# TensorE's products as one loop of eight rounds, in a batched matrix product that the DMA queue bounds

## The chip, the cores and the metric

One core of a Trainium2 chip. The metric is the device time of one execution in microseconds, as the median of several. The four executions of the kernel before took 134.46 to 134.86 us, a range of 0.3%. The times of one table were taken on the same chip in the same rounds.

## The reference, cut to what matters

```python
batch, dim_i, dim_j, dim_k = 32, 256, 512, 384
x: (batch, dim_i, dim_j) float32        # 16.8 MB
y: (batch, dim_j, dim_k) float32        # 25.2 MB
out = np.einsum('bij,bjk->bik', x, y).astype(np.float32)   # 12.6 MB
```

## The kernel before

The kernel works on eight groups of four matrices. For each group, SyncE issues the loads of x and y; VectorE rounds x to 16 bits (2.29 us for 128 x 4096), transposes it (2.00 us for 128 x 1024 as 32-bit elements), and rounds y (0.95 us for 128 x 1536); TensorE makes 128 products; ScalarE (and VectorE for one or a few banks) copies the sums out of PSUM; SyncE stores the group. All data transfers go through one queue (q1, 54.53 MB), which the 16 DMA engines share: the trace has 16 completion writes for each of the 24 loads and stores, which are taken here as 16 shares, one for each engine.

```python
PLAN = """
x0 x1 y0
T0 x2 y1
T1 R0 M0 C0 x3 y2
T2 D0 R1 M1 C1 x4 y3
...                                   # cut: the same pattern
T6 D4 R5 M5 C5 y7
T7 D5 R6 M6 C6 R7 M7 C7 D7 S3 S4 S5 S6 S7
"""
x_pool, y_pool, yr_pool: bufs=2;  xr_pool: bufs=1;  xt_pool: bufs=3;  o_pool: bufs=5   # cut to sizes

def multiply(n):                      # M: one group's products, written out for every n
    for e in range(NE):               # NE = 2 halves
        for t in range(T):            # T = 16
            for g in range(Q):        # Q = 4 matrices, each on 32 partitions
                nc.tensor.matmul(ps_of[n, e, g], xt[s, e, t // 2, :, t % 2], y_r[s, t],
                                 start=(t == 0), stop=(t == T - 1))

def collect(n, vector):               # C on ScalarE, D on VectorE: PSUM -> o_sb
    ...
def store(n):                         # S: one DMA of 1.5 MB
    ...
```

The framework (a scheduler with pools of buffers) places the waits; nothing in TensorE's program branches back. TensorE's program is therefore 8 x 128 products, each with a weight load (1,024 of each on the page).

## Time and profile before

| | before |
|---|---|
| time, median of 3 | 134.52 us (134.51 to 134.86) |
| span of the profiled execution | 132.9 us |
| busiest compute engine | VectorE, 72% |
| the data queue's share of the 16 DMA engines' time | 96.9% |
| fetches of TensorE's instructions | 8, of 16 KiB each |

Read it from the queue's share down: here one resource is at 97% and every engine at 72% or less, so only that resource, and the two ends of the run where it is not yet or no longer busy, can give time. The lines of the page that show this stand in the prediction below, each with what is to be seen in it.

The trace records, for every load or store, 16 small completion writes of the DMA engines (384 of 4 bytes for the 24 transfers). I number the transfers 0 (first load) to 23 (last store, S7), and call "lateness" of an engine the time of its write less that of the first engine's write for the same transfer. The writes do not name their engine. A row of lateness is therefore sorted, and that a value in one row and a like value in the next belong to the same engine is inferred.

### The profile page before, as it was taken

To read this page: it belongs to the slowest core of one execution; us is meant where nothing else is said; L and a number is where in the kernel's file an instruction comes from. 1 tells how busy PE (TensorE), PEld (TensorE's weight loads), DVE (VectorE), ACT (ScalarE), POOL (GpSimd) and SP (SyncE) were. 2 spreads that over 40 slices of the span, in tenths; PEclk is the share of its full clock that TensorE was granted. 3 is DMA by queue.
4 is the path that set the end of the run, shared out by engine and by line. 5 is a ranking of instruction groups with operands and counts; after the bars stand their busy time and mean duration, and the time that the engine had idled before them with its cause. 6 is when DMAs were issued, how large, how long until landed. Compare 5 with 4: busy or idle time off the path is not lost.

```text
span 132.9 us, 2437 instructions
## 1 busy us (share of the span) xinstructions
PE 61.5 (46%) x1024; PEld 34.9 (26%) x1024; DVE 96.1 (72%) x92; ACT 91.7 (69%) x193; POOL 0.2 (0%) x4
## 2 busy tenths in 40 slices
PE   0000004990399129924952395329540079887100
PEld 0000002550147014612541153115320034455000
DVE  0049999699959999999997999699951090735600
ACT  3000000089999999999999999999999961998500
POOL 0000000000000000000000000000000000000000
PEclk9999999999658975797799869985999555999955
DMA  4999999999999999999999999999999999999993
GB/s 109 429 424 441 451 414 429 446 429 412 419 471 407 404 437 441 432 409 446 429 417 414 456 432 402 414 419 429 429 464 429 414 451 400 419 425 412 400 412 141
DMA packets 3723, 54.68 MB, mean 412 GB/s; under 512 B 384, under 2 KB 384, under 8 KB 896
## 3 DMA queue, kind: packets, MB, share of 16 engines
q1 hardware_dynamic: 3712, 54.53, 96.9%
q8 instruction: 8, 0.13, 0.4%
q14 instruction: 3, 0.02, 0.0%
HBM read 41.94 MB, written 12.58 MB: 410 GB/s over the span
## 4 chain that ended last, share of the span: by engine, by line
DMA 45%; DVE 19%; ACT 15%; PE 10%; issue 4%; DVEq 1%
DMA x_sb<-in_x_dram 22%; DMA y_sb<-in_y_dram 22%; ACT o_sb L153 15%; PE o_ps L132 10%; DVE xt_sb L113 6%; DVE x_r L106 5%; DVE o_sb L153 4%; DVE y_r L119 4%; DVEq L202 1%; DVEq L106 0%
## 5 line engine op out<-in xcount | busy, mean ns | idle before, releaser
L153 ACT COPY o_sb<-o_ps 32x384 f32<-32x384 f32 (+1 forms) x192 | 90.4, 471 | 32.7 <-PE o_ps L132 25.8
L132 PE MATMUL o_ps<-y_r,xt_sb 32*128 32x384 f16 x1024 | 61.5, 399 | 61.7 <-DVE y_r L119 52.3
L132 PEld LDWEIGHTS <-xt_sb 32*128 32x128 f16 x1024 | 34.9, 113 | 87.9 <-DVE y_r L119 32.8
L119 DVE CAST y_r<-y_sb 128x1536 f16<-128x1536 f32 x32 | 28.5, 953 | 10.3 <-DMA y_sb<-in_y_dram 10.2
L113 DVE STREAM_TRANSPOSE xt_sb<-x_r 128x1024 f32<-128x1024 f32 (+1 forms) x20 | 31.7, 1631 | 0.3
L106 DVE CAST x_r<-x_sb 128x4096 f16<-128x4096 f32 x8 | 18.3, 2292 | 11.1 <-DMA x_sb<-in_x_dram 11.0
L153 DVE COPY o_sb<-o_ps 32x384 f32<-32x384 f32 (+1 forms) x32 | 17.8, 556 | 7.8 <-PE o_ps L132 3.8
L153 ACT ACT_TABLE_LOAD x1 | 1.3, 1283 | 0.7 <-PEq L191 0.7
L191 POOL MEMSET const-uint8-127<- 128x1 uint8 x1 | 0.1, 103 | 0.0
L191 POOL MEMSET const-bfloat16-1.0<- 128x1 bf16 x1 | 0.1, 102 | 0.0
L191 POOL MEMSET const-float32-0.0<- 128x1 f32 x1 | 0.1, 99 | 0.2 <-issue 0.2
L191 POOL MEMSET const-float32-1.0<- 128x1 f32 x1 | 0.1, 99 | 0.0
## 6 DMA issues: line engine op xcount, KB each, us to landing
y_sb<-in_y_dram SPq DMA_DIRECT2D x8, 3072.0 KB, 21.5
x_sb<-in_x_dram SPq DMA_DIRECT2D x8, 2048.0 KB, 22.0
out_dram<-o_sb SPq DMA_DIRECT2D x8, 1536.0 KB, 25.6
```

The source lines that it names most:

```text
L106: keep(nc.vector.tensor_copy(x_r, x_of.pop(n)))
L113: keep(nc.vector.transpose(dst[:, c, e], src[:, c, e]))
L119: keep(nc.vector.tensor_copy(yr_of[n][:, a : a + STEP], y_sb[:, a : a + STEP]))
L132: nc.tensor.matmul(ps_of[n, e, g], xt[s, e, t // 2, :, t % 2], y_r[s, t], start=(t == 0), stop=(t == T - 1),)
L153: keep(copy(o[a : a + w, g // per, h * NE + e], ps[h * w : (h + 1) * w]))
L191: nc = _bacc.Bacc("TRN2", target_bir_lowering=False, num_devices=1)
L202: with _tile.TileContext(nc) as tc:
```

## The change

Its intent: TensorE's code becomes one body of 128 products, run eight times, so that its instructions need not be fetched eight times. To serve a loop, transposed x and rounded y become one buffer each (the body is written once, with fixed buffers), so VectorE waits for products before it overwrites; group 7's transposed x goes to a spare buffer and is copied across. The loaded x gets three buffers (two before), and VectorE copies two banks of group 6, where before ScalarE copied them all. All waits are written by hand on semaphores in one section. VectorE's copies of group n-1 go ahead of the rounding of x of group n+1. The waits for the stores move behind the section.

```diff
-    xt_pool = ctx.enter_context(tc.tile_pool(name="xt_pool", bufs=3))
-    yr_pool = ctx.enter_context(tc.tile_pool(name="yr_pool", bufs=2))
+    y_r = pool.tile([P, T, K], MM_DT, name="y_r")
+    xt = pool.tile([P, NE, TW, P], F32, name="xt_sb")
+    xt_spare = pool.tile([P, NE, TW, P], F32, name="xt_spare")
...
+    x_in = [sem(f"x_in_{n}") for n in range(N)]        # ... 43 semaphores in all at the end, 11 before
...
+        eng.reg_mov(count, 0)
+        eng.br_lt(count, 0, on_true="products_loop", on_false="products_next")   # always jumps over the body
+        with nc.body("products_loop", valid_engines=(PE,)):
+            n1 = eng.snap(count, min_val=1, max_val=N)
+            for e in range(NE):
+                eng.wait_ge(act_done[e], n1)
...
+                        i = eng.matmul(bank[e, g], w[s, e, t // 2, :, t % 2], y_r[s, t],
+                                       start=(t == 0), stop=(t == T - 1))
...
+            eng.br("products_next")
+        with nc.body("products_next", valid_engines=(PE,)):
+            eng.reg_add(count, count, 1)
+            eng.br_lt(count, N + 1, on_true="products_loop", on_false="products_end")
...
+    with tc.tile_critical():
+        queue(LOADS)
+        tensor()
+        queue(QUEUE)
+        scalar()
+        vector()
+    tc.no_sync_barrier()
...
+    for n in reversed(range(N)):
+        nc.sync.wait_ge(o_out[n], landed)
```

(The 43 and 11 are the author's counts of the semaphores that the last clear of each kernel covers; no trace shows a count. "..." marks cuts.)

## The prediction

> **What bounds the kernel now.** I read the page's slices first, because they say which resource never rests, then its queues, then the table of stretches for the two ends, then the groups and the waits.
>
> ```profile
> span 132.9 us, 2437 instructions
> ...
> PE 61.5 (46%) x1024; PEld 34.9 (26%) x1024; DVE 96.1 (72%) x92; ACT 91.7 (69%) x193; POOL 0.2 (0%) x4
> ...
> DMA  4999999999999999999999999999999999999993
> ...
> q1 hardware_dynamic: 3712, 54.53, 96.9%
> q8 instruction: 8, 0.13, 0.4%
> q14 instruction: 3, 0.02, 0.0%
> ```
>
> No compute engine is over 72% busy, while the DMA row is at 9 in every slice but the first and last. The data are fixed: 41.9 MB read, 12.6 MB written. The table of stretches (the last two columns are DMA share and GB/s) shows where the transfers run at their rate and where not:
>
> ```profile
> 0.00:2.00 2.00, 0.00 (x0) 0.00 (x0) 0.00 (x0) 1.27 (x1) 0.20 (x4) 1.00 0.44 82
> 2.00:4.00 2.00, 0.00 (x0) 0.00 (x0) 0.00 (x0) 0.01 (x1) 0.00 (x0) 1.00 0.69 229
> 4.00:28.00 24.00, 6.22 (x84) 3.55 (x88) 18.22 (x12) 0.90 (x2) 0.00 (x0) 1.00 1.01 433
> ...
> 98.00:124.00 26.00, 14.46 (x256) 7.96 (x256) 12.27 (x18) 20.62 (x44) 0.00 (x0) 0.80 1.00 423
> 124.00:126.00 2.00, 0.00 (x0) 0.00 (x0) 1.49 (x3) 1.05 (x3) 0.00 (x0) 1.00 0.98 412
> 126.00:128.00 2.00, 0.00 (x0) 0.00 (x0) 0.00 (x0) 0.00 (x0) 0.00 (x0) 0.63 0.94 390
> ...
> 130.00:132.00 2.00, 0.00 (x0) 0.00 (x0) 0.00 (x0) 0.00 (x0) 0.00 (x0) 0.50 0.33 138
> ```
>
> From 4 to 124 us the 16 DMA engines are full at 423 to 433 GB/s. What is not a full-rate transfer lies at the ends: first packets at 1.8 us, a ramp to 4 us, a shortfall near 126 us and a ragged finish after 130 us. So only the ends and the bytes can give anything; about 127 us (54.53 MB at 430 GB/s, worked out) can't be moved by this change.
>
> (Names as in the kernel's plan: x6 and y6 are the loads of group 6, X, T, R the rounding of x, its transposes and the rounding of y on VectorE, C and D the copies out of PSUM by ScalarE and VectorE, S7 the store of group 7.)
>
> The raggedness has a shape. In the trace each transfer ends in 16 completion writes, one per DMA engine. Over the first four transfers they spread over 0.65 us. The first instruction fetch starts at 30.49 us (16 KiB, 1.05 us in one packet); from the next completion on the spread is 2.2 us, and stays 2.0 to 2.3 us to the store before last (125.71 to 128.00 us). One or more engines fell about 1.55 us behind at the fetch and never caught up, since none had idle time. Later fetches (45.5, 58.2, 71.6, 85.4, 99.1, 116.2, 122.2 us) don't widen the spread, as if each fell on another engine. The last transfer ends on the laggard, at 131.70 us; the first engine was done at 130.25.
>
> The end of the kernel, per instruction in the trace: SyncE gets past the last store's wait at 132.07 us and the closing barriers end at 132.88. The run is 134.52 us, 1.6 us over the span; I keep that constant.
>
> ```profile
> L119 DVE CAST y_r<-y_sb 128x1536 f16<-128x1536 f32 x32 | 28.5, 953 | 10.3 <-DMA y_sb<-in_y_dram 10.2
> L113 DVE STREAM_TRANSPOSE xt_sb<-x_r 128x1024 f32<-128x1024 f32 x12 | 23.6, 2001 | 0.2
> L106 DVE CAST x_r<-x_sb 128x4096 f16<-128x4096 f32 x8 | 18.3, 2292 | 11.1 <-DMA x_sb<-in_x_dram 11.0
> L153 ACT COPY o_sb<-o_ps 32x384 f32<-32x384 f32 x168 | 79.0, 470 | 27.6 <-PE o_ps L132 25.1
> ```
>
> These durations are my prices. ScalarE runs without a break from 27 to 108 us: 28 copies of 0.48 us (with the gap) are 13.5 us a group, so ScalarE paces the middle, though behind the DMA queue, which is always fed.
>
> [...]
>
> **The change part by part.**
> The loop. TensorE's 2,050 listed instructions become one body of 128 products (256 with weight loads) run eight times. If the body stays in the instruction memory, most of the eight fetches go. Mean load removed: 8 x 1.05 / 16 = 0.5 us per DMA engine; but the end is set by the laggard, so the gain is the spread that vanishes: 2.2 - 0.65 = 1.55 us. Engines without a fetch gain nothing from it, but they were held up at the end: S7 was issued at 125.58, and with about 0.9 us to first packets the early engines stood idle from 125.7 to 126.5.
>
> So S7 must come earlier to cash the gain. Tail, from ScalarE and TensorE: y6 is in near 105.8; VectorE finishes round x7 and half of its transpose near 106 and rounds y6 by 109.5. Group 6's first half runs cold from 106.9 for 5.3 us (before: 107.23 to 112.6) to 112.2, its second half to 115.0. ScalarE: 8 copies to 116.05, and 6 (VectorE now takes two of group 6) to 118.95, where before it was 8, to 120.45. VectorE: the two spare copies[...], y7 rounded 113 to 117, D6 (2 x 0.556) done by 118.8. Group 7's second half then starts at 118.95 instead of 120.50 and ends at 121.75; VectorE's last two copies of each pair end at 124.0. S7 issue: 124.1, 1.5 us earlier; packets at 125.0, before any DMA engine is out of work at 125.7. End of the transfers: 131.70 - 1.55 = 130.15.
>
> The middle. y_r and the transposed x are now one buffer each, so rounding waits for products. Let C(n-1) end at t: second half of n until t+2.8, transpose to t+4.8, rounding y from there, first quarter at t+5.75; the next group's products wait for ScalarE's t+7.7 anyway and, cold, end at t+13.0, before ScalarE is free at t+13.5. The period stays 13.5 us, with 0.5 us to spare; and y6's landing gives 4 to 5 us more in all. Loads are asked for no later: y6 after R4 (75.6 against 76.6), y7 after R5 (89.1 against 90.2). Copies ahead of rounding x thus cost no path.
>
> The start. A no-op, a wait and a second branch stand ahead of the first load[...], +0.17. The end: the stores' waits, now after the section, are in one group that S7 ends, plus one branch: +0.07; the section's own closing lies before the landing and is hidden.
>
> Sum: 134.52 - 1.55 + 0.17 + 0.07 = 133.21; I say 133.3, for a remaining fetch or two.
>
> **The rivals.** (a) The loop refetches[...]. Then there are 8 to 16 fetches as before, the spread stays[...]: 134.5 to 135.[...] Against it: only that the change pays with two single buffers for the loop, which only fewer fetches would repay. I give it 30%. (b) VectorE becomes the bound, since the single buffers tie it to TensorE: 12 us a group of work against 13.5. It needs over 4 us lost in all before the queue or the tail sees it: 135 to 138. The DMA queue's lead of over 11 us at each y load speaks against it. (c) The gain is larger, through a better ramp or no spread at all: even a zero spread gives 134.52 - 2.2 + 0.24 = 132.6. Against a 2% gain (131.8) stands the transfers' rate.
>
> **Range and chances.** 70% near 133.2 with 0.4 either way, 30% at 134.5 or over: 133.3, range 132.4 to 134.9. Faster by over 2% needs under 131.8, below even (c): 4%. Slower by over 2% needs rival (b): 4%. Within 2%: 92%.
>
> **What would show it.** Right: the instruction queue's line falls from 8 packets to one or two; completion spread under 1 us to the end; S7 issued near 124 us; no dip at 126 us; DMA row 9 from 4 to 129 us. Wrong: as many fetches or more, with TensorE idle at each round's start for no engine (rival a); a DMA digit under 9 in the middle, or VectorE waiting on products and ScalarE with gaps (b); first packets after 2.1 us would make the start's term wrong.

## The result, and the profile after

| | before | after |
|---|---|---|
| median of the same rounds | 134.51 us (134.46 to 134.86, 4 runs) | 135.33 us (135.04 to 135.52, 4 runs) |
| ratio of the fast runs | | 1.0054, 95% interval 1.0029 to 1.0079 |

A ratio here and below is the mean time of the one kernel's fast runs over that of the other's fast runs in the same rounds, so it is not quite the ratio of the medians that are quoted. The change made the kernel a little slower: within 2%, but above the predicted range of 132.4 to 134.9.

The page of the kernel after:

```profile
span 133.6 us, 2502 instructions
...
DMA  4999999999999999999999999999999999999980
...
q1 hardware_dynamic: 3712, 54.53, 96.3%
...
q8 instruction: 1, 0.02, 0.0%
```

The first thing to see is that the change did what it was for: TensorE's instruction queue, q8, went from 8 packets and 0.13 MB to 1 packet and 0.02 MB. (That q8 is TensorE's is read from the runs: 8 packets with the products written out, 1 with the loop, no line at all in fewprod and fewest below.) And it bought nothing: the span is 0.7 us longer. The stretches of the kernel after (engines' busy times, granted clock, DMA share, GB/s):

```profile
0.00:2.00 2.00, 0.00 (x0) 0.00 (x0) 0.00 (x0) 0.90 (x1) 0.20 (x4) 1.00 0.17 41
...
124.00:126.00 2.00, 0.00 (x0) 0.00 (x0) 0.72 (x2) 0.36 (x1) 0.00 (x0) 0.91 1.02 427
126.00:128.00 2.00, 0.00 (x0) 0.00 (x0) 0.00 (x0) 0.00 (x0) 0.00 (x0) 0.50 0.98 412
128.00:130.00 2.00, 0.00 (x0) 0.00 (x0) 0.00 (x0) 0.00 (x0) 0.00 (x0) 0.50 0.88 369
130.00:132.00 2.00, 0.00 (x0) 0.00 (x0) 0.00 (x0) 0.00 (x0) 0.00 (x0) 0.50 0.17 71
```

The shortfall near 126 us is gone in this trace (412 GB/s; before 390), as predicted; the second pair below shows that this was chance. But from 130 to 132 us the DMA engines are still 17% busy: some two to three of the 16 work on, alone. Before, that stretch stood at 33%. So most engines are now done sooner, and the last ones later.

The completion writes say the same more sharply. This is the lateness of the 16 engines, sorted, in us, before the last store (transfer 22), worked out from the trace's records:

```
before  0 .08 .15 .36 .45 .98 1.18 1.22 1.36 1.44 1.67 1.67 1.69 1.78 1.98 2.30
after   0 .08 .23 .23 .24 .26  .27  .33  .37  .42  .55  .67 1.12 1.82 2.29 2.76
```

Before, eight engines are between 1.3 and 2.3 us late. After, 12 of 16 are within 0.7 us of the first, and four are not. The mean lateness fell from 1.14 to 0.73 us (sum of each row over 16; in the second pair below from 1.21 to 0.70), close to the 0.5 us of fetch per engine that the prediction worked out. The largest did not fall.

Where the 0.7 us of the span went, for the first pair of traces and for a second pair (both kernels run again in later rounds):

| us | before | after | before again | after again |
|---|---|---|---|---|
| first load issued | 0.73 | 0.94 | 0.73 | 0.94 |
| first packet | 1.79 | 1.96 | 1.78 | 1.96 |
| first to last packet | 129.91 | 130.23 | 129.89 | 129.58 |
| last packet to the end | 1.17 | 1.40 | 1.27 | 1.51 |
| span | 132.88 | 133.58 | 132.94 | 133.05 |
| latest engine before S7 | 2.30 | 2.76 | 2.24 | 2.12 |
| S7 issued | 125.58 | 124.81 | 124.47 | 125.57 |
| GB/s from 126 to 128 us | 390 | 412 | 415 | 372 |

The start (+0.17 and +0.18) and the closing (+0.23 and +0.24) are nearly the same in both pairs. The transfers are not: +0.32 in one pair, -0.31 in the other. Either way they did not get the 1.55 us shorter that the prediction rested on. The last two rows go with the execution and not with the kernel: each kernel has one trace with a late S7 and a shortfall, and one with neither.

The middle went as predicted. ScalarE copies without a break, in one run of 168 copies, as before (start, duration, then what it waited for at its start):

```profile
27.61 80.98 ACT L142 COPY o_sb<-o_ps 32x384 f32<-32x384 f32 x168 [25.22 <-PE o_ps L231]
```

and TensorE shows a slow ("cold") first half of 5.3 us, a second half of as many products in 2.8 us (the granted clock was 0.52 from 48.86 to 54.13 us and 1.00 from 54.65 to 57.43 us), and 4.9 us of waiting for ScalarE (in brackets) between groups:

```profile
48.86 5.27 PE L231 MATMUL o_ps<-y_r,xt_sb 32*128 32x384 f16 x64 [4.94 <-ACT o_sb L142]
54.65 2.78 PE L231 MATMUL o_ps<-y_r,xt_sb 32*128 32x384 f16 x64 [0.52 <-ACT o_sb L142]
62.36 5.30 PE L231 MATMUL o_ps<-y_r,xt_sb 32*128 32x384 f16 x64 [4.93 <-ACT o_sb L142]
```

The two slow halves shown start 13.50 us apart: the period that the prediction worked out. No engine waits for an instruction fetch that the timeline shows.

### The profile page after: what moved, and what is told of

The parts are those of the page before. It is cut to its first block, busy times and chain, and to the rows that moved or that the text cites.

```text
span 133.6 us, 2502 instructions
## 1 busy us (share of the span) xinstructions
PE 60.4 (45%) x1024; PEld 31.3 (23%) x1024; DVE 98.8 (74%) x96; ACT 90.6 (68%) x191; POOL 0.2 (0%) x4
## 4 chain that ended last, share of the span: by engine, by line
ACT 54%; DMA 15%; PE 11%; DVE 8%; issue 4%; SPq 1%
ACT o_sb L142 54%; DMA y_sb<-in_y_dram 15%; PE o_ps L231 11%; DVE o_sb L142 3%; DVE x_r L163 2%; DVE y_r L196 1%; DVE xt_spare L177 1%; DVE xt_sb L177 1%; SPq L107 1%; SPq L286 0%; SPq L248 0%
## 5 line engine op out<-in xcount | busy, mean ns | idle before, releaser
L142 ACT COPY o_sb<-o_ps 32x384 f32<-32x384 f32 (+1 forms) x190 | 89.3, 470 | 32.7 <-PE o_ps L231 30.3
L231 PE MATMUL o_ps<-y_r,xt_sb 32*128 32x384 f16 x1024 | 60.4, 402 | 62.1 <-DVE y_r L196 33.0
L231 PEld LDWEIGHTS o_ps<-y_r,xt_sb 32*128 32x128 f16 x1024 | 31.3, 113 | 90.7 <-issue 44.9
L177 DVE STREAM_TRANSPOSE xt_sb<-x_r 128x1024 f32<-128x1024 f32 (+1 forms) x16 | 28.2, 1784 | 5.6 <-PE o_ps L231 5.5
L142 DVE COPY o_sb<-o_ps 32x384 f32<-32x384 f32 (+1 forms) x34 | 18.9, 556 | 1.2 <-PE o_ps L231 0.6
L177 DVE STREAM_TRANSPOSE xt_spare<-x_r 128x512 f32<-128x512 f32 x4 | 4.2, 1085 | 0.0
L183 DVE COPY xt_sb<-xt_spare 128x2048 f16<-128x2048 f16 x2 | 1.4, 690 | 0.5 <-PE o_ps L231 0.5
```

The source lines that it names most:

```text
L142: i = copy(o[a : a + w, g // per, h * NE + e], bank[e, g][h * w : (h + 1) * w])
L177: i = eng.transpose(dst[:, c, e], src[:, c, e])
L183: eng.tensor_copy(xt.bitcast(MM_DT)[:, e], xt_spare.bitcast(MM_DT)[:, e]).then_inc(x_ready[e], 1)
L231: i = eng.matmul(bank[e, g], w[s, e, t // 2, :, t % 2], y_r[s, t], start=(t == 0), stop=(t == T - 1),)
```

## The experiments

**What is to be told apart.** The theories, by the names that the expectations use:

(N, G and V are explained where the expectations use them.)

- L, latest engine: each transfer is complete when the slowest of 16 engines has done its share. The shares are fixed, so an engine that has once fallen behind keeps its lateness as long as the queue is full (in the kernel before, 2.21 us at the first fetch and 2.30 us before S7). The end follows the one latest engine. One fetch makes one engine late; eight fetches make up to eight engines about equally late. Removing seven of eight gives the last of them nothing.
- F, the fetches: the lateness at the end is the fetches' alone, so a kernel without a TensorE fetch should gain the full 1.5 us.
- Rival reasons for the slower time: the section's start and closing, the new order on VectorE, the place of the stores' waits.

L2 is the form of L in which, behind the engine that the fetch made late, others stand that are late for other reasons.

### The two kernels again, with and without the loop, and without its first jump

*b_again* is the kernel before, *a_again* the kernel after, unchanged. *unroll* takes the loop out and keeps all else:

```diff
-        eng.reg_mov(count, 0)
-        eng.br_lt(count, 0, on_true="products_loop", on_false="products_next")
-        with nc.body("products_loop", valid_engines=(PE,)):
-            n1 = eng.snap(count, min_val=1, max_val=N)
+        for n1 in range(1, N + 1):
```

*noskip* keeps the loop and removes the forward jump over its body:

```diff
-        eng.reg_mov(count, 0)
-        eng.br_lt(count, 0, on_true="products_loop", on_false="products_next")
+        eng.reg_mov(count, 1)
+        eng.br("products_loop")
```

(and the block products_next becomes the end of the body).

> The kernel before once more, for a second trace. Both theories: 134.5 us. If the place where an instruction fetch falls is fixed, the spread of the 16 completion writes grows again from 0.65 to about 2.2 us at the first fetch near 30 us and ends at 2.2 to 2.4 us before the last store; if it is chance, the latest DMA engine ends the store before last 1.2 to 4 us after the first one.

> The changed kernel once more, for a second trace. Theory L (the latest of the 16 DMA engines sets the end, and it is the one that takes TensorE's single fetch at 4.2 us): 135.3 us, one engine 1.7 us late from the very first load, 2.5 us or more at the end, twelve engines within 0.7 us. Rival N (fetches don't matter, the loss is all at the start and in the closing): same time, but the engine that ends last is another one than that which was late at the first load.

> The changed kernel with its products written out eight times in place of the loop; all else is kept. Theory L: eight fetches return near the groups' ends, none at 4 us, so the first loads' spread is 0.7 us; several engines are 1.5 us late, the last one 2.3 us; the transfers end as in the kernel before but 0.2 us later for the later start: 134.9 to 135.1 us, so 0.2 to 0.4 us faster than the loop. Rival G (fewer fetches do help, by the 0.5 us of mean load): 135.8 us, 0.5 us slower than the loop.

> The loop entered from above: no forward jump over the body at the start, the counter starts at 1. Theory L with the jump as the cause of the fetch at 4.2 us: that fetch moves to the end of the first round (near 30 us) or goes; first loads' spread 0.7 us. If it only moves, the engine it falls on is still 1.5 us late later and the time stays within 0.3 us of the changed kernel's; if it goes, the latest engine is 0.9 to 1.2 us earlier: 134.2 us. Rival N: no change of the time in either case.

| | median us | ratio to before | TensorE fetches | latest engine before S7 |
|---|---|---|---|---|
| before, same rounds | 134.33 | | | |
| b_again | 134.38 | 1.0001 (0.9985 to 1.0016) | 8 | 2.24 |
| a_again | 134.89 | 1.0049 (1.0033 to 1.0066) | 1, at 4.2 us | 2.12 |
| unroll | 134.95 | 1.0049 (1.0033 to 1.0065) | 8 | 2.25 |
| noskip | 134.80 | 1.0033 (1.0021 to 1.0046) | 1, at 30.4 us | 2.20 |

The queues of unroll:

```profile
q1 hardware_dynamic: 3712, 54.53, 96.7%
q8 instruction: 8, 0.13, 0.4%
```

Unroll has seven fetches more than the loop and takes the same time; that it would be some tenths faster was a miss. So the loop by itself costs nothing and gains nothing that these runs can tell: seven fetches of about 1 us each are worth zero here, to within some 0.3 us (the two intervals). The loss of 0.5% sits in what unroll and the loop share.

The one fetch left is caused by the loop's first jump. It comes at 4.2 us, while the first load is under way, and the first piece of work pays for it. VectorE's first instruction, in the kernel before, after, and in noskip (in brackets the wait for x0):

```profile
8.41 2.29 DVE L106 CAST x_r<-x_sb 128x4096 f16<-128x4096 f32 x1 [8.41 <-DMA x_sb<-in_x_dram]
```

```profile
9.76 2.29 DVE L163 CAST x_r<-x_sb 128x4096 f16<-128x4096 f32 x1 [9.76 <-DMA x_sb<-in_x_dram]
```

```profile
8.61 2.29 DVE L163 CAST x_r<-x_sb 128x4096 f16<-128x4096 f32 x1 [8.61 <-DMA x_sb<-in_x_dram]
```

A fetch of 0.93 us on one of 16 engines made x0 land more than 1.1 us later: of the 16 landings of x0 in the kernel after, the 15th is recorded at 8.53 us and the last at 9.73 us, and VectorE starts at 9.76 us. Without the jump the fetch is not avoided, it moves to 30.4 us, and the latest engine at the end is as late as ever.

A_again missed in part what L expected: 134.89 us in place of 135.3, and 2.12 us at the end in place of 2.5 or more. By these four times alone rival N (fetches do not matter, the loss is at the start and in the closing) is not refuted; whether the engine that ends last is the one that was late at the first load can't be read, since the writes do not name it. Skew and fewprod below tell L from N.

### One loop body in less code, wider copies, and a block meant to be jumped over

*fits* (on noskip; a wrong result) leaves out most products of the fourth matrix, so that the body has some 210 instructions in place of 256. *wide64* (on noskip, correct) copies PSUM on 64 partitions in every group, for fewer ScalarE and VectorE instructions. *fits_w64* is both. *jumpy* (on after, correct) puts a block of 128 products that never runs between body and counter; each round was to jump over it.

```diff
 fits
+                        if g == Q - 1 and t < T - 1:
+                            continue
-                            start=(t == 0),
+                            start=(t == 0 or g == Q - 1),
 wide64
-NARROW_GROUPS = (6, 7)
+NARROW_GROUPS = (0, 1, 2, 3, 4, 5, 6, 7)
 jumpy
+        with nc.body("products_dead", valid_engines=(PE,)):
+            ...                                   # 128 matmuls, never entered
+            eng.br("products_next")
```

> Wrong result on purpose: the loop entered from above, with all but one of the 16 products of each fourth batch left out, so that the body has about 210 instructions instead of about 270[...]. If TensorE then fetches nothing while data move: Theory F (TensorE's fetch alone held the end): the 16 completion writes stay within 0.8 us, 133.4 to 133.6 us. Theory L2 (the latest engine holds the end, and there are more causes of lateness than TensorE's fetch: [...]one engine that loses 0.3 us in each store of 12,288-byte packets): the spread is still 1.8 to 2.1 us at the end, 134.5 to 134.8 us, at most 0.3 us below the run with the loop entered from above (134.80 us).

> The loop entered from above and all groups with 64-partition copies and stores of 6,144-byte packets, as groups 6 and 7 have them: half as many copies on ScalarE. Theory L2: the engine that lost 0.3 us in each store no longer does[...], TensorE's one fetch still makes one engine 1.8 us late; each store costs all engines 0.06 us more, 0.36 us in all: 134.6 to 135.0 us. Theory F: the same time or 0.3 us more.

> Wrong result on purpose: both of these at once, the short body and the 64-partition copies. Theory L2: no late engine is left, spread 1 us or less at the end; 1.2 us gained, 0.36 us paid for smaller packets: 133.6 to 134.1 us, though each of the two alone gained next to nothing. If something else holds the end: 134.5 us or more.

> The changed kernel with a block of 128 products that never runs between the loop's body and its end, so that each round jumps forward over more than 256 instructions and back. Theory L: two or more fetches a round, 16 or more in all, so some engine takes two or more; the latest is 3 us or more behind at the end and the time rises by 1 to 3 us, 136 to 138 us[...]. Rival G (mean load): 16 more fetches of 1 us over 16 engines, 1 us more. If the instruction memory holds all of it: no change, 134.9 us.

| | median us (before: 134.37) | ratio to before |
|---|---|---|
| fits | 135.17 (134.40 to 136.52) | 1.0052 (1.0027 to 1.0078) |
| wide64 | 135.50 | 1.0084 (1.0068 to 1.0100) |
| fits_w64 | 135.31 | 1.0080 (1.0062 to 1.0098) |
| jumpy | 135.18 | 1.0057 (1.0040 to 1.0073) |

Three misses. Fits was to lose its fetch and did not: one still came, at 46.8 us, in the second round. Its profiled run was slow (granted clock 0.73), so nothing is concluded from its time. Wide64 was to remove an engine that falls some 0.3 us further behind at each store; one engine was still 2.58 us late before S7, and the kernel was slower than noskip. (The 0.06 us a store that it was to pay is what the kernel before shows: 460 ns for a packet of 12,288 bytes and 234 ns for one of 6,144, by medians, so 8 against 16 packets on an engine.) In fits_w64 a fetch came at 44.2 us and the latest engine stayed 2.25 us late. Since neither cause was in fact removed, these three say only that the latest engine and the time stayed high together. Why a fetch came in the second round is open.

Jumpy was to settle a rival, and does not. Its queues:

```profile
span 133.4 us, 2502 instructions
...
q1 hardware_dynamic: 3712, 54.53, 96.5%
q8 instruction: 1, 0.02, 0.0%
```

There is one fetch in all, and by its expectations that would mean that a jump over the block costs no fetch. But the trace holds no jump. TensorE's records show a compare-and-branch at the end of each round, in the kernel after and in jumpy alike, and none between the body and the counter. The counter's first instruction starts 16 to 20 ns after the start of the round's last product, against 15 to 18 ns in the kernel after and 16 to 22 in noskip, where nothing stands between. So the dead block was not in the path, and jumpy is one more run of the kernel after. What refutes the prediction's rival (a), a refetch at every branch back, is the kernel after itself: TensorE's trace has seven branches back between the rounds, of 0.21 us each, and one fetch. How long a body can become before it is fetched again was not tried.

### The same bytes on two engines or on all, the stores' waits, VectorE's order

*skew* (on after, correct) adds 20 small loads of two rows of 5,120 B each (0.2 MB together), spread through the run, whose data nobody uses; S7 waits for them. *even* adds the same 0.2 MB as two loads of 128 rows of 800 B.

```diff
+        def extra(n):
+            if n >= 3:
+                eng.wait_ge(z_in[n % 3], 16 * (n // 3))
 skew
+            eng.dma_start(out=z_all[0:2, n % 3], in_=<2 rows of 1280 of x[n]>).then_inc(z_in[n % 3], 16)
 even
+            eng.dma_start(out=z_all[:, n % 3, 0:200], in_=<128 rows of 200 of x[n]>).then_inc(z_in[n % 3], 16)
```

*inside* puts the waits for the stores back into the section; *dorder* rounds x of group n+1 ahead of the copies of group n-1:

```diff
 inside
+        if "S7" in steps:
+            for n in reversed(range(N)):
+                eng.wait_ge(o_out[n], 16)
-    tc.no_sync_barrier()
-    ...                                           # and the waits behind the section
 dorder
-X0 T0 R0 X1 T1 R1 D0 X2 T2 R2 D1 X3 T3 R3 ... D4 X6 T6 D5 X7 U7
+X0 T0 R0 X1 T1 R1 X2 D0 T2 R2 X3 D1 T3 R3 ... X6 D4 T6 X7 D5 U7
```

(The place that D had in the kernel before, behind the transposes, would deadlock with one buffer for transposed x, so it was not tried.)

> The changed kernel and 20 extra loads of two rows of 5,120 bytes, one after nearly every load and store, to a spare place: 0.2 MB in all. If such a load goes to two DMA engines only and always to the same ones, these two get some 4 us more of work (20 x 0.2 us), the other 14 none. Theory L (the latest engine sets the end): two engines 4 us or more behind at the end, and the time rises by 2 to 4 us over the changed kernel's 134.9: 137 to 139 us. Rival G (the mean load counts): 0.2 MB at 430 GB/s are 0.5 us: 135.4 us. If the engines change from load to load: each gets about 0.5 us, 135.4 us under both.

> Control for the extra loads on two engines: the same 0.2 MB as two loads of 128 rows of 800 bytes, which fall on all 16 engines alike. Both theories: 0.5 us more than the changed kernel, 135.3 to 135.5 us, and the spread at the end as without them (2.1 to 2.8 us).

> The changed kernel with its waits for the stores undone: back inside the section, as constants. The section's closing (0.4 us between its first and last step in the changed kernel's trace, then hidden ahead of the landing) now comes after the last landing, and the register wait and its branch go: from the last landing to the end 1.4 to 1.5 us in place of 1.4 with the present order (0.35 + 1.05 us): +0.3 us, 135.2 us. If the closing is hidden in either place: 134.9 us.

> The changed kernel with VectorE's order undone where that can be: x of group n+1 is rounded before group n-1 is copied out. (Behind the transposes, as in the kernel before, it can't stand: the transposes would wait for products that wait for this copy.) Theory: VectorE is no bound and the DMA queue is 11 us ahead, so the time stays within 0.2 us of the changed kernel's 134.9 us, and TensorE's second half of each group starts up to 2.3 us later at most where ScalarE isn't later anyway. Rival V (VectorE's order sets the pace): slower by 0.5 us or more, with gaps on ScalarE.

| | median us (before: 134.34) | ratio to before |
|---|---|---|
| skew | 139.36 (139.06 to 139.65) | 1.0367 (1.0350 to 1.0384) |
| even | 135.46 (135.28 to 135.61) | 1.0083 (1.0068 to 1.0097) |
| inside | 135.36 (135.14 to 135.79) | 1.0074 (1.0062 to 1.0086) |
| dorder | 134.83 (134.66 to 136.15) | 1.0069 (1.0033 to 1.0105) |

Skew against even is the decisive pair for L: the same bytes, the same compute, 3.9 us apart. Skew's DMA row, its extra loads (count, size), and two stretches of its end:

```profile
DMA  4999999999999999999999999999999999969490
...
z_sb<-in_x_dram SPq DMA_DIRECT2D x20, 10.0 KB
```

```profile
128.00:130.00 2.00, 0.00 (x0) 0.00 (x0) 0.33 (x1) 0.00 (x0) 0.00 (x0) 1.00 0.13 55
...
134.00:136.00 2.00, 0.00 (x0) 0.00 (x0) 0.00 (x0) 0.00 (x0) 0.00 (x0) 0.50 0.11 46
```

A share of 0.13 is two engines of 16 (0.125), and each extra load has two completion writes. Each of the two engines got 20 packets of 196 ns (median; mean 214), so 3.9 to 4.3 us of work: the whole difference in time, which came out just above the 137 to 139 us that L expected. They run alone twice: from 128 us, when the other 14 have nothing left because the last loads, and so S7 (issued at 129.16 us), came late through the same two engines; and again from 134 us, until S7's last shares are written. In even, whose 288 packets more than the kernel after are 256 rows and 16 completion writes for each of the two loads, the same stretches are

```profile
128.00:130.00 2.00, 0.00 (x0) 0.00 (x0) 0.00 (x0) 0.00 (x0) 0.00 (x0) 0.50 1.01 424
130.00:132.00 2.00, 0.00 (x0) 0.00 (x0) 0.00 (x0) 0.00 (x0) 0.00 (x0) 0.50 0.31 129
```

The queue never caught up for the late pair, though the mean load of skew's engines is that of even's.

Inside is some 0.3 us slower than the loop as it was (1.0074 against 1.0049 and 1.0054), as expected, though the intervals overlap; its closing after the last packet is 1.93 us, against 1.40 and 1.51. So moving the stores' waits behind the section was, by these single traces, the right part of the change. Dorder is the same as the loop within its wide interval, which one run of its four, 1.3 us above the others, makes so wide. Its median is 0.1 us below a_again's, so no loss from the new order on VectorE is seen; a tenth or two can't be excluded. Not tested by themselves: the third buffer for x and group 6's copies on VectorE.

### No TensorE fetch at all

*fewprod* (on noskip; a wrong result) keeps 11 of 128 products a round, just those that signal something, some 55 TensorE instructions in all with their waits and weight loads; no fetch for TensorE is recorded then. *fewest* also copies each bank in one instruction of 128 partitions, for fewer instructions on ScalarE and VectorE. *noskip2* is noskip again, beside them.

```diff
 fewprod, fewest
+                        if t < T - 1 and not (e == NE - 1 and g == 0 and t % STEP == STEP - 1):
+                            continue
-                            start=(t == 0),
-                            stop=(t == T - 1),
+                            start=True,
+                            stop=True,
 fewest
-            for h in range(per):
-                i = copy(o[a : a + w, g // per, h * NE + e], bank[e, g][h * w : (h + 1) * w])
+            i = copy(o_all[:, n % O_BUFS, g * NE + e], bank[e, g])
```

> Wrong result on purpose: the loop entered from above with 11 products a round in place of 128, so that TensorE's whole program is about 55 instructions and it has nothing to fetch while data move. Copies, loads and stores as in the changed kernel. Theory F (TensorE's one fetch alone keeps the latest engine late): spread under 1 us up to the last store, and 133.4 to 133.8 us. Theory L2 (other late engines stand behind it): the spread before the last store is 1.3 to 2.1 us, from three fetches of 8 KiB and the engine that loses time in the stores: 134.2 to 134.8 us.

> Wrong result on purpose: as before, and each PSUM bank copied out by one copy of 128 partitions in place of two or four, so that ScalarE too has about 75 instructions in place of 212; the stores keep their packets. Theory L2 with instruction fetches as the only cause: none or one fetch of 8 KiB in the trace, spread under 1 us: 133.3 to 133.7 us. If the engine that loses 0.3 us in each store of 12,288-byte packets is a thing of its own: the spread still grows to 1.5 to 2 us during the stores, 134.2 to 134.7 us.

> The loop entered from above once more, with right results, beside the two above on the same chip. One fetch near 30 us, spread 2.0 to 2.3 us, 134.7 to 134.9 us.

| | median us (before: 134.38) | ratio to before | latest engine before S7 | first to last packet |
|---|---|---|---|---|
| fewprod | 134.25 | 0.9987 (0.9974 to 1.0000) | 1.55 | 129.12 |
| fewest | 134.14 | 0.9987 (0.9974 to 1.0000) | 1.09 | 128.80 |
| noskip2 | 135.04 | 1.0047 (1.0032 to 1.0062) | 2.16 | 129.95 |

The pages of fewprod and of fewest; there is no line of TensorE's queue q8 in either:

```profile
span 132.5 us, 643 instructions
...
q1 hardware_dynamic: 3712, 54.53, 97.0%
q14 instruction: 4, 0.02, 0.0%
```

```profile
span 132.2 us, 483 instructions
...
q14 instruction: 2, 0.02, 0.0%
```

Fewprod gains 0.8 us on noskip2, half of what F needs: F falls, L2 stands. Fewest fits neither of its stated outcomes exactly, and its median is only 0.1 us below fewprod's, though its trace has the latest engine 0.46 us earlier. The lateness, sorted, before S7:

```
noskip   0 .05 .12 .14 .23 .24 .32 .34 .40 .42 .45 .53 1.35 1.47 2.05 2.20
fewprod  0 .05 .17 .20 .22 .24 .29 .33 .38 .38 .38 .41  .51  .58 1.41 1.55
fewest   0 .05 .12 .18 .22 .23 .25 .25 .27 .28 .31 .35  .36  .74  .81 1.09
```

Taking away TensorE's fetch uncovers the next engines. What they carry is in the traces: fetches of 8 KiB by the other instruction queue, q14, of 0.3 us in one packet (near 48, 75 and 117 us in the loop kernels), after which one engine stands some 0.7 to 1.2 us later than before (a new value in the sorted rows; which engine's code q14 fetches is not shown); and in the kernels with all their products one engine that falls back some 0.3 us at each store, for no recorded reason (in the kernel after, a value of 0.46, 0.72 and 1.08 us in the rows of the first three stores). A caution: fewprod and fewest also take nearly all of TensorE's work away, not the fetch alone, so part of their gain may be something else. No correct kernel without the fetch was found.

With these, L can be checked as a sum. Take the first-to-last-packet time less the latest engine's lateness before S7; if L holds it is one constant:

```
             first to last packet - latest engine = rest
before             129.91           2.30    127.61
b_again            129.89           2.24    127.65
after              130.23           2.76    127.47
a_again            129.58           2.12    127.46
unroll             129.73           2.25    127.48
noskip             129.73           2.20    127.53
wide64             130.32           2.58    127.74
fewprod            129.12           1.55    127.57
fewest             128.80           1.09    127.71
noskip2            129.95           2.16    127.79
```

The first column ranges over 1.5 us, the rest over 0.3 us. The other kernels with the same bytes lie in the same range (127.5 to 127.8), but for fits, whose trace is slow. The sum is less free than it looks: the rest is what the first engine needs up to its write before S7 (123.8 to 124.1 us) plus what the latest engine needs for its share of S7, 3.70 or 3.71 us in each of these traces. What it shows is that the latest engine goes from the transfer before straight to S7 and ends the run, whether S7 was issued at 120.14 us (fewest) or at 125.58.

### The closing: how many semaphores are cleared

After the last store has landed (132.06 us in the kernel before), GpSimd clears the kernel's semaphores between two barriers (semaphore records of all engines at 132.4 and again at 132.8 us). The record in the kernel before and after (duration in ns three times, as least, median and largest of one; then its time in us):

```profile
L202 POOLq EVENT_SEMAPHORE_RANGE_CLEAR  x1: 95/95/95, 132.5 to 132.5; - x1
```

```profile
L286 POOLq EVENT_SEMAPHORE_RANGE_CLEAR  x1: 268/268/268, 133.0 to 133.0; - x1
```

That is 173 ns for 32 semaphores more by the author's count, 5.4 ns each. Two kernels on noskip change only the number: *sems_more* allots 64 that nothing uses, *sems_less* shares the loads' semaphores by buffer.

```diff
 sems_more
+    unused = [sem(f"unused_{n}") for n in range(64)]
 sems_less
-    x_in = [sem(f"x_in_{n}") for n in range(N)]
-    y_in = [sem(f"y_in_{n}") for n in range(N)]
+    x_in = [sem(f"x_in_{n}") for n in range(X_BUFS)]
+    y_in = [sem(f"y_in_{n}") for n in range(Y_BUFS)]
...                                               # waits count up by 16 for each use
```

> The loop without the initial jump (noskip), plus 64 semaphores that nothing uses: 107 in place of 43 to clear at the end. If the clear that GpSimd makes of the kernel's semaphores costs by their number and lies on the path after the last store (95 ns for 11, 268 ns for 43 in the traces: 5.4 ns each), its record reads about 615 ns, and the run takes 0.35 us more than noskip: 135.1 to 135.4, with the closing after the last packet 1.75 to 1.85 us. If the clear is hidden beside the barriers, or costs by something else, the time stays at 134.8 to 135.0.

> The same loop with the loads' semaphores shared by buffer (5 in place of 16): 32 to clear in place of 43. By semaphores: the record falls by 11 x 5.4 = 60 ns to about 208 ns and the time by 0.06 us, which the timing can't tell from noskip (134.75 to 135.0), so this run speaks by its record alone. Nothing here should beat the kernel before (about 134.35).

Their records:

```profile
L285 POOLq EVENT_SEMAPHORE_RANGE_CLEAR  x1: 615/615/615, 132.8 to 132.8; - x1
```

```profile
L284 POOLq EVENT_SEMAPHORE_RANGE_CLEAR  x1: 207/207/207, 133.2 to 133.2; - x1
```

| | median us (before: 134.45) | ratio to before | last packet to the end |
|---|---|---|---|
| sems_more (107 to clear) | 135.29 (135.06 to 135.48) | 1.0054 (1.0037 to 1.0070) | 1.84 |
| sems_less (32 to clear) | 134.81 (134.53 to 135.51) | 1.0014 (0.9997 to 1.0030) | 1.42 |

The expected records were 615 and about 208 ns, the expected closing of sems_more 1.75 to 1.85 us. So the clear costs by number (95 ns for 11, 207 for 32, 268 for 43, 615 for 107, so about 36 ns and 5.4 ns for each), and sems_more shows that it lies on the path to the end (its closing is 1.84 us): the 75 semaphores between the two kernels are 0.41 us by the records, 0.42 us by the closings and 0.48 us by the medians. The 11 fewer of sems_less are too few to see: its closing is 1.42 us where noskip's is 1.40. Of the closing's +0.23 us in the kernel after, 0.17 is this.

Nothing measured here that computes the right result beats the kernel before. The best of the loop kernels, noskip and sems_less, are at 134.80 and 134.81 us with 134.33 and 134.45 for the kernel before in the same rounds; sems_less can just not be told from it.

## Why the prediction was wrong, point by point

**What bounds the kernel** was right: the DMA row stayed full, and only the ends moved.

**The fetches: right.** "If the body stays in the instruction memory, most of the eight fetches go": 8 became 1 (where the body is kept between rounds, the trace does not show).

**The gain from them: the step that failed.** "Mean load removed: 8 x 1.05 / 16 = 0.5 us per DMA engine; but the end is set by the laggard, so the gain is the spread that vanishes: 2.2 - 0.65 = 1.55 us." The first half was right, and the mean lateness did fall by 0.41 us (1.14 - 0.73; 0.51 in the second pair). The conclusion does not follow from the prediction's own reading. It had seen that the first fetch alone made the spread of 2.2 us, and that later ones "don't widen the spread, as if each fell on another engine". Then the last seven fetches were worth nothing, and one remaining fetch keeps the whole loss. Yet it allowed "a remaining fetch or two" and took 0.1 us off for them. Measured: a spread of 2.12 to 2.76 us in place of 0.65, transfers of 129.58 to 130.23 us in place of 128.4 (129.91 - 1.55). Unroll against the loop shows the worth of seven fetches, none; skew against even shows the mechanism; fewprod shows that without any TensorE fetch the gain is still about half, because other engines are next in line.

**The tail: mis-sized, and without effect.** Group 7's second half was predicted at 118.95 us and S7 at 124.1. The chain of waits of the kernel after has the half

```profile
119.64 2.84 PE o_ps L231 x64
```

where the kernel before had it at 120.50; S7 was issued at 124.81 (125.57 when run again; before 125.58 and 124.47). That the dip at 126 us vanished in the first trace was luck: it stands in the second trace of the kernel after and not in the second of the kernel before. The end did not follow it. The trace of the kernel after with the late S7 has the shorter transfers, 129.58 against 130.23 us, since an earlier S7 only feeds engines that are early; the latest is still busy with older work at that moment (in the first trace S7 was issued at 124.81 us, and the latest engine's write for the transfer before came at 128.48 us).

**The start: right.** Predicted +0.17 us; the first load is issued as shown (start, duration, for the first two loads), before and after,

```profile
0.73 0.87 SPq L87 DMA_DIRECT2D x_sb<-in_x_dram  x2
```

```profile
0.94 0.87 SPq L107 DMA_DIRECT2D x_sb<-in_x_dram  x2
```

and the first packet moved from 1.79 to 1.96 us. The price behind it is less sure than the sum. The trace of the kernel before records no branch, so the +0.17 us, and the +0.07 us at the end with its one branch more, were estimates; recorded compare-and-branches in the kernel after took 33 ns (SyncE, entering the section) and 207 ns (TensorE, each branch back).

**The closing: mis-sized.** Predicted +0.07 us, measured +0.23 and +0.24. The missing term was 32 more semaphores to clear, 0.17 us; the sems kernels show it.

**The middle: right.** The period was 13.5 us, and the two spare copies took 0.69 us each (page, count, busy, mean ns):

```profile
L183 DVE COPY xt_sb<-xt_spare 128x2048 f16<-128x2048 f16 x2 | 1.4, 690 | 0.5 <-PE o_ps L231 0.5
```

**The rivals.** (a), refetching each round, was refuted by the queue's line (one fetch in eight rounds); its number, 134.5 to 135, lay near the truth for another reason. (b), VectorE as the bound, did not happen. The outcome itself, fewer fetches with the same spread, was named as nobody's rival, although the prediction's own reading of the spread contained it.

**The sum again.** With the failed term at about zero on average, start and closing give 0.39 to 0.42 us of loss, where the two timed comparisons of the unchanged loop (0.82 and 0.56 us by medians) and unroll (0.62) show some 0.6 to 0.8. The other 0.2 to 0.4 must, by subtraction, lie in the transfers, where single traces scatter by 0.7 us (129.58 to 130.23 for the same kernel); which engine carries it in a typical run is open. Open as well: why a fetch of 1.05 us sets an engine back by 1.55 us (0.66 to 2.21 us at the first fetch of the kernel before), why one engine falls back at each store, and why the latest engine falls back once more during the load of y7 (near 105 to 111 us), with no fetch recorded there: from 1.86 to 2.76 us in the first trace of the kernel after, 2.01 to 2.30 before, 1.80 to 2.20 in noskip, and not at all in b_again and unroll.

## What to carry to other kernels

In a kernel that keeps all DMA engines busy, read the lateness of each engine, not the mean load. Here a transfer ended with its latest share (x0 in the kernel after at 9.73 us, with 15 of 16 in by 8.53 us), the fixed shares did not rebalance while the queue was full (2.21 us late at the first fetch of the kernel before, 2.30 us before S7), and taking away work that lay on many engines paid only down to the next latest one (noskip 2.20, fewprod 1.55, fewest 1.09 us). Before you price the removal of n like events, ask what the first of them costs alone; if one already makes the whole loss, removing all but one is worth nothing. Count semaphores and section entries too: here the fixed costs at start and end (0.4 us) were larger than what the loop bought.
